# A two-layer diffusion backbone on one core: another order in the opening, at the layer boundaries and in the second mixing stage

## The chip, the core and the metric

The kernel runs on one core of a Trainium2 chip. The metric is the time of one execution on the device, in microseconds (us). Its median before the change is 2162.36 us over three runs (2161.0 to 2166.12).

## What is computed

Two streams of tokens pass through two layers: 256 latent tokens `x` (called X below) and 256 context tokens `ctx` (called H), each 1024 wide. The reference, cut to what matters:

```
for l in range(2):
    mod_x = silu(c) @ ada_w[l] + ada_b[l]        # 9 vectors of 1024: shifts, scales, gates
    mod_h = silu(c_ctx) @ ada_w[l] + ada_b[l]
    x, h += 0.5 * mod[2] * swiglu(modulated(x, h; mod, norm_g[l, 0]), ffa)
    sx, sh = mixer_streams(modulated(x, h; mod, norm_g[l, 1]), w_in[l], ...)
    x += mod_x[5] * mixer_output(sx, keys of h and x)   # MLA, differential attention, pooling, three gates
    h likewise, in layer 0 alone
    x, h += 0.5 * mod[8] * swiglu(modulated(x, h; mod, norm_g[l, 2]), ffb)   # h in layer 0 alone
return rmsnorm(x, final_g)

modulated(z) = rmsnorm(z, g) * (1 + scale) + shift
```

The change leaves all of this as it is; only the order of the work and some of its forms differ.

## The kernel before, in words

**Layout.** The residual stream lies as eight tiles `X[k]` of 128 features by 512 tokens; columns 0 to 255 (`XC`) are X, 256 to 511 (`HC`) are H. Every product is made in three passes from a high part and a low part of each operand (`mm3`, line 301): `wh*xh`, `wh*xl`, `wl*xh`. TensorE (PE) works through instructions in the order in which the program issues them, and so does every other engine.

**Weights.** Weights come from HBM as 406 chunks of 128x1024 (eight blocks of 128x128). `Weights.split` (line 152 and 156) loads a chunk, ACT rounds it to the high part `hi`, and POOL or DVE subtracts to get the low part `lo`. `k.pool_split(n)` says which of the two; the markers `P` and `D` in a schedule and `on_pool` set it. A ring holds four chunks.

**The opening** (`start`, from line 1420). The two conditioning rows are loaded into rows 0 and 1 of `crow` and go through Silu. PE makes three products of ones to have work (`warm`), transposes the rows into columns (`pa`), and broadcasts each row over 128 partitions by four products `cb` whose operands have two rows (line 1484). DVE and ACT square the tiles `X[k]` and add them; PE sums these over partitions (`total`, tile `pst`), the first slice of the modulation matrix is multiplied by the conditioning columns (`prod`, line 1508), ACT copies the broadcast rows to `cvec` (`wide`), DVE makes row products for the shifts (`shifts`, line 1519), and when the scales (`fin`), the root of the mean square (`rs`) and its broadcast `rB` are there, DVE and ACT make the modulated input (`ut` line 409, `uh` line 412, `ul` line 419). Then the first products `fg`, `fu` of the first FFN start (line 1578).

**The boundaries** (`boundary`, four of them: before each mixing stage, before the second FFN of layer 0, before the first FFN of layer 1). The last four output tiles of the stage before are finished for H first and then for X, so that H can be normalised while X is still being finished. `sqacc` squares an updated tile on ACT and adds it to `acc`, on POOL, and for the last tile on DVE (line 371). `stat` sums `acc` over partitions on PE (line 381, tile `pst`), ACT takes the root, DVE the reciprocal; `bcast` spreads it (line 396, `rB`). The next stage's first products ("items", `fg` and `fu` of the first two column groups of an FFN; `dk0`, `dq0`, `dv0` of a mixing stage) run for H alone: item 0 whole, then `xstat` for X, then item 1, with the broadcast and the modulation of X issued in its middle, then the rest; after that they run for X. A `W.hold` keeps their weights in the ring for the second pass.

**The mixing stages.** `SCHEDULE[l]` is an order written out by hand: twelve attention units in layer 1 (eight differential, four MLA), and behind each the names of the work that PE does before the next unit: projections (`dk`, `dq`, `kv`, `cq`, `q`, `k`), `v0`/`v1`, gates `g..`, transposes `T`, products with values `V`, statistics `ls` and `st` with `sq`, and `N` for a softmax step on DVE and POOL. A unit's scores (`sc`, lines 790 and 1118) fill four of the eight PSUM banks; DVE takes the maxima, ACT the exponentials, and then the banks are free.

Of the kernel before, what the change touches and what calls it, by code (L numbers as in the profile page):

```python
# [84 lines left out]
class Weights:  # L85


    def __init__(self, k, stream):
        self.k = k
        self.stream = stream  # L90
        self.c, self.off = -1, CW
        self.done = 0
        self.floor = None
        self.look = RING - 1
        self.hi, self.lo = {}, {}
        self.blocks = []
        self.early = {}
        self.jobs = [n for a, b in EARLY for n in range(a, b)]
        self.loaded = self.parted = None
        self.plain = 0  # L100

# [38 lines left out]
    def split(self, n, parts, copy):  # L140
# [13 lines left out]
        for p in range(parts):  # L154
            c = slice(p * CW // parts, (p + 1) * CW // parts)
            eng.tensor_tensor(out=lo[:, c], in0=raw[:, c], in1=hi[:, c].bitcast(F32), op=ALU.subtract)  # L156
# [6 lines left out]
    def prefetch(self, n, parts=1, copy=None):  # L163
        while self.done < NSPLIT and self.done <= n:
            self.split(self.done, parts, copy or self.k.nc.scalar.copy)
            self.done += 1
# [24 lines left out]
class Kernel:  # L191
# [274 lines left out]
    def boundary(self, l, i, specs, xs, update, head, func):  # L466
# [15 lines left out]
        for dm in g:  # L482
            banks[dm] = self.ps("dn")
            blks[dm] = self.gemm(banks[dm][:, HC], specs(dm), xs, HC)
            update(dm, banks[dm], HC)
            self.sqacc(dm, HC, nc.vector if dm == KD - 1 else None)
# [3 lines left out]
        for n, dm in enumerate(g):  # L490
            self.gemm(banks[dm][:, XC], blks[dm], xs, XC, mids[n])
            update(dm, banks[dm], XC)
            self.sqacc(dm, XC, nc.vector if dm == KD - 1 else None)
# [7 lines left out]
        def xstat():  # L501
            self.stat(X_)
            self.preload(func)
        for n, it in enumerate(items):
            it.mm(H_, lambda: (self.bcast(X_), self.mod_list(X_, range(KD)), self.mod_end()) if n == 1 else None)
            if n == 0:
                xstat()
# [920 lines left out]
    def start(self):  # L1428
# [6 lines left out]
        crow = self.pt("crow", F32).rearrange("p a b -> p (a b)")  # L1435
        nc.sync.dma_start(crow[0:2, :], cvec)
        nc.sync.dma_start(self.cst0, cst[:, 0:NK0])
# [45 lines left out]
        for (s, h), p in bc.items():  # L1483
            nc.tensor.matmul(p, self.ident[0:2, s:s + 1].to_broadcast([2, 128]), crow[0:2, h * 512:h * 512 + 512],
                             start=True, stop=True)

        def wide(s, copy):
            for h in range(2):
                copy(self.cvec[:, s, h * 512:h * 512 + 512], bc[s, h])
# [42 lines left out]
        for k in range(0, KD, 2):  # L1532
# [3 lines left out]
            if k == 2:  # L1536
                add(0, 2)
                total(0)
        prod(0, 1)
        wide(H_, act.copy)  # L1540
        dve.scalar_tensor_tensor(out=ab1, in0=self.v(V_ADAB + 8, 8), scalar=1.0, in1=self.v(V_NORM, 8),
                                 op0=ALU.add, op1=ALU.mult)
        total(4)
        turn(0, 1)
        total(6)
        shifts(0, H_)
        r, r2 = self.sm("rs", 4), self.sm("rs2", 4)
        act.activation(r, pst[:, 0:4], AF.Sqrt, scale=1.0 / D, bias=self.eps)
        dve.reciprocal(r2, r)
        wide(X_, act.copy)  # L1550
        fin(0, 1)
        p = self.ps("rB")
# [3 lines left out]
        shifts(0, X_)  # L1556
# [31 lines left out]
        self.W.prefetch(0)  # L1588
# [181 lines left out]
```

## Time and profile before

| | before |
|---|---|
| median of three runs | 2162.36 us |
| the profiled execution, its own time | 2161.61 us |
| its span, first to last instruction | 2159.8 us |
| mean granted clock of PE, as a share of full | 0.991 |
| PE busy | 2120.6 us (98%) |
| DVE, ACT, POOL busy | 63%, 42%, 36% |
| DMA, mean | 189 GB/s |

The span is what the trace covers; the profiled execution's own time is 1.8 us more. PE's busy time counts products that overlap, so 98% does not say that PE works at its peak; the 39 us in which it is not busy are real holes, and a stretch in which its granted clock is below 1.00 is slower work. In rows of instructions the columns are start, duration, engine, line, operation, tiles written and read, shapes, count; in brackets the idle time of that engine just before and what ended it.

### The profile page before, as it was taken

To read this page: it belongs to the slowest core of one execution; us is meant where nothing else is said; L and a number is where in the kernel's file an instruction comes from. 1 tells how busy PE (TensorE), PEld (TensorE's weight loads), DVE (VectorE), ACT (ScalarE), POOL (GpSimd) and SP (SyncE) were. 2 spreads that over 40 slices of the span, in tenths; PEclk is the share of its full clock that TensorE was granted. 3 is DMA by queue.
4 is the path that set the end of the run, shared out by engine and by line. 5 is a ranking of instruction groups with operands and counts; after the bars stand their busy time and mean duration, and the time that the engine had idled before them with its cause. 6 is when DMAs were issued, how large, how long until landed. Compare 5 with 4: busy or idle time off the path is not lost.

```text
span 2159.8 us, 31295 instructions
## 1 busy us (share of the span) xinstructions
PE 2120.6 (98%) x12032; PEld 1824.9 (84%) x12032; DVE 1370.3 (63%) x2016; ACT 899.7 (42%) x1529; POOL 772.2 (36%) x561
## 2 busy tenths in 40 slices
PE   9999999999999999999999999999999999999998
PEld 5888888977887788888888898888889888999998
DVE  6665655456656799468758745544534776667755
ACT  4433233345565533432212243332333557555544
POOL 0333324322475411555545544333343347301000
PEclk9999999999999999999999999999999999999999
DMA  7577767264322466245444515786664552455653
GB/s 265 184 292 278 256 265 273 86 217 142 113 93 80 150 234 234 88 145 181 172 166 166 175 69 209 294 299 237 264 246 147 205 185 79 166 200 191 229 183 115
DMA packets 119241, 408.91 MB, mean 189 GB/s; under 512 B 13234, under 2 KB 16946, under 8 KB 119092
## 3 DMA queue, kind: packets, MB, share of 16 engines
q1 hardware_dynamic: 103252, 354.48, 46.7%
q10 hardware_dynamic: 15840, 52.44, 6.2%
q8 instruction: 94, 1.54, 0.3%
q14 instruction: 55, 0.45, 0.1%
HBM read 348.67 MB, written 58.20 MB: 188 GB/s over the span
## 4 chain that ended last, share of the span: by engine, by line
PE 86%; DVE 6%; ACT 4%; issue 1%; DMA 1%; POOL 1%; ACTq 0%; DVEq 0%; SPq 0%; POOLq 0%
PE dn L301 22%; PE fu L301 19%; PE fg L301 19%; PE gt L301 8%; PE it L301 5%; PE br L301 5%; PE vi L301 2%; ACT pe L806 1%; DVE ul L419 1%; PE fg L1578 1%; PE fu L1578 1%; PE pa L1508 1%; PE tr L853 1%; PE sc L1118 1%; DMA X<-X 1%
## 5 line engine op out<-in xcount | busy, mean ns | idle before, releaser
L156 POOL TENSOR_TENSOR lo<-w,hi 128x1024 fp32r<-128x1024 f32 x204 | 530.4, 2603 | 701.3 <-ACT hi L152 652.9
L152 ACT CAST hi<-w 128x1024 fp32r<-128x1024 f32 x359 | 374.8, 1049 | 579.2 <-DMA w<-in_stream 237.6
L271 DVE CUSTOM_DVE_ANT_0 junk<-a,cvec 128x1024 bf16<-128x1024 f32 x224 | 400.5, 1788 | 3.7
L301 PE MATMUL dn<-hh,hi 128*128 128x512 f32 (+1 forms) x800 | 272.7, 341 | 0.0
L301 PE MATMUL dn<-hl,hi 128*128 128x512 f32 (+1 forms) x800 | 272.2, 340 | 0.0
L301 PE MATMUL dn<-hh,lo 128*128 128x512 f32 (+1 forms) x800 | 272.2, 340 | 0.0
L156 DVE TENSOR_TENSOR lo<-w,hi 128x1024 fp32r<-128x1024 f32 x155 | 190.5, 1235 | 127.9 <-ACT hi L152 125.5
L301 PE MATMUL fg<-ul,hi 128*128 128x512 f32 (+2 forms) x712 | 252.4, 354 | 1.6 <-DVE ul L419 1.6
L301 PE MATMUL fu<-uh,hi 128*128 128x512 f32 (+2 forms) x712 | 253.8, 357 | 0.0
L301 PE MATMUL fu<-ul,hi 128*128 128x512 f32 (+2 forms) x712 | 253.2, 356 | 0.0
L301 PE MATMUL fu<-uh,lo 128*128 128x512 f32 (+2 forms) x712 | 253.1, 355 | 0.0
L301 PE MATMUL fg<-uh,hi 128*128 128x512 f32 (+2 forms) x712 | 251.7, 354 | 0.0
L301 PE MATMUL fg<-uh,lo 128*128 128x512 f32 (+2 forms) x712 | 251.5, 353 | 0.0
L301 PEld LDWEIGHTS dn<-hh,hi 128*128 128x128 f32 x800 | 151.7, 190 | 17.0
L301 PEld LDWEIGHTS dn<-hl,hi 128*128 128x128 f32 x800 | 151.7, 190 | 16.8
L301 PEld LDWEIGHTS dn<-hh,lo 128*128 128x128 f32 x800 | 151.7, 190 | 16.9
L619 DVE SCALAR_TENSOR_TENSOR X<-dn,md,X 128x256 f32<-128x256 f32 x112 | 50.2, 479 | 170.6 <-PE dn L301 170.5
L301 PEld LDWEIGHTS fg<-ul,hi 128*128 128x128 f32 x712 | 134.4, 189 | 21.1 <-DVE ul L419 2.8
L301 PEld LDWEIGHTS fu<-uh,hi 128*128 128x128 f32 x712 | 136.4, 192 | 18.5
L301 PEld LDWEIGHTS fu<-ul,hi 128*128 128x128 f32 x712 | 136.4, 192 | 18.4
L301 PEld LDWEIGHTS fu<-uh,lo 128*128 128x128 f32 x712 | 136.2, 191 | 18.3
L301 PEld LDWEIGHTS fg<-uh,lo 128*128 128x128 f32 x712 | 134.5, 189 | 18.5
(321 smaller groups left out, 4303.2 us busy)
## 6 DMA issues: line engine op xcount, KB each, us to landing
w<-in_stream SPq DMA_DIRECT2D x359, 512.0 KB, 4.2
a<-in_ada SPq DMA_DIRECT2D x136, 512.0 KB, 4.4
el<-in_stream SPq DMA_DIRECT2D x47, 512.0 KB, 3.7
early<-eh ACTq DMA_DIRECT2D x47, 512.0 KB, 2.7
early<-el ACTq DMA_DIRECT2D x47, 512.0 KB, 3.7
hi<-early SPq DMA_DIRECT2D x47, 512.0 KB, 4.4
lo<-early SPq DMA_DIRECT2D x47, 512.0 KB, 5.8
a<-in_stream SPq DMA_DIRECT2D x8, 512.0 KB, 6.6
```

The lines of the kernel that those rows point to most:

```text
L152: copy(hi, raw)
L156: eng.tensor_tensor(out=lo[:, c], in0=raw[:, c], in1=hi[:, c].bitcast(F32), op=ALU.subtract)
L271: nc.vector.tensor_tensor_reduce(out=self.junk, in0=raw, in1=self.cvec[:, s, :], scale=1.0, scalar=0.0, op0=ALU.mult, op1=ALU.add, accum_o ...
L301: nc.tensor.matmul(out, a, b, start=first and n == 0, stop=last and n == 2)
L419: self.nc.vector.scalar_tensor_tensor(out=lo, in0=t, scalar=sh, in1=hi.bitcast(F32), op0=ALU.add, op1=ALU.subtract)
L619: nc.vector.scalar_tensor_tensor(out=x, in0=p[:, SC[s]], scalar=K.mod(self.l, m, s, dm), in1=x, op0=ALU.mult, op1=ALU.add)
L806: nc.scalar.activation(e[:, c], banks[i][:, c], AF.Exp, bias=nm[:, o:o + 1], scale=1.0, accum_out=ls[:, o:o + 1])
L853: nc.tensor.transpose(t[:, i * 128:i * 128 + 128], P[:, i * 128:i * 128 + 128], self.ident)
L1118: nc.tensor.matmul(out[qt], a[0:96, q0:q0 + 128], b[0:96, kc], start=n == 0, stop=n == 2)
L1508: nc.tensor.matmul(pa[0:2, c], ccol[:, 2 * i:2 * i + 2], ada[k, m][:, i * 128:i * 128 + 128], start=i == 0, stop=i == KD - 1)
L1578: nc.tensor.matmul(b, w[n // 2], x, start=k == n == 0, stop=k == KD - 1 and n == 2)
```

## The change

What it does, in the order of the program:

- `SCHEDULE[1]`, the order of the mixing stage of layer 1, is another one.
- `Weights.split` on POOL makes the low part in two halves of 128x512 (`parts=2`); on DVE it stays one instruction. In the opening the low part can be issued later than the high part (`lows`).
- `sqacc` for the last tile of a boundary no longer adds on DVE: the square stays apart (`sq7`) and `stat` sums both tiles on PE.
- `boundary`: where the first two items that take H are ordinary ones, they run together for H, block by block, with `xstat` after the sixth and the X broadcast and modulation after the eighth block. The boundary before layer 1's mixing has only one such item and keeps the old form.
- `start`: `crow` is zeroed (half on POOL, half on DVE) before its DMA, which is now behind that of `cst0`; the broadcasts `cb` use all 128 rows; two more `warm` products; the copies `wide`, the sums `total`, the X row product `shifts(0, X_)` and the rounding of the first chunk are issued earlier.

```diff
--- before.py
+++ after.py
@@ -48,11 +48,11 @@
...
-    "N dk1 dq1 | N P kv0 cq0 | N | N N N N N T kv1 N N N V D dk2 N N N dq2 N T N N N | N N cq1 | N cq2 dk3 N N P "
...
+    "dk1 dq2 N | N P N N N dq1 cq0 kv0 | P N T kv1 N | N N | dk2 N N N N D N N dk3 N N T N N dq3 cq1 N N N V N "
...
@@ -98,6 +98,7 @@
         self.jobs = [n for a, b in EARLY for n in range(a, b)]
         self.loaded = self.parted = None
         self.plain = 0
+        self.lows = None
 
     def plain_chunk(self, specs):
 
@@ -151,16 +152,24 @@
         nc.sync.dma_start(raw, self.stream[n])
         copy(hi, raw)
         eng = nc.gpsimd if k.pool_split(n) else nc.vector
-        for p in range(parts):
-            c = slice(p * CW // parts, (p + 1) * CW // parts)
-            eng.tensor_tensor(out=lo[:, c], in0=raw[:, c], in1=hi[:, c].bitcast(F32), op=ALU.subtract)
+        if eng is nc.vector:
+            parts = 1
+
+        def low():
+            for p in range(parts):
+                c = slice(p * CW // parts, (p + 1) * CW // parts)
+                eng.tensor_tensor(out=lo[:, c], in0=raw[:, c], in1=hi[:, c].bitcast(F32), op=ALU.subtract)
+        if self.lows is None:
+            low()
+        else:
+            self.lows.append(low)
         self.hi[n], self.lo[n] = hi, lo
 
     def pump(self):
         floor = self.c if self.floor is None else min(self.floor, self.c)
         self.prefetch(floor + self.look)
 
-    def prefetch(self, n, parts=1, copy=None):
+    def prefetch(self, n, parts=2, copy=None):
         while self.done < NSPLIT and self.done <= n:
             self.split(self.done, parts, copy or self.k.nc.scalar.copy)
             self.done += 1
@@ -483,14 +492,14 @@
             banks[dm] = self.ps("dn")
             blks[dm] = self.gemm(banks[dm][:, HC], specs(dm), xs, HC)
             update(dm, banks[dm], HC)
-            self.sqacc(dm, HC, nc.vector if dm == KD - 1 else None)
+            self.sqacc(dm, HC, False if dm == KD - 1 else None)
         mids = (None, lambda: (self.bcast(H_), self.mod_list(H_, (0, 1))),
                 lambda: self.mod_list(H_, (4, 5)), lambda: self.mod_end())
         ends = ((), (2, 3), (6, 7), ())
         for n, dm in enumerate(g):
             self.gemm(banks[dm][:, XC], blks[dm], xs, XC, mids[n])
             update(dm, banks[dm], XC)
-            self.sqacc(dm, XC, nc.vector if dm == KD - 1 else None)
+            self.sqacc(dm, XC, False if dm == KD - 1 else None)
             if n == 0:
                 self.stat(H_)
             self.mod_list(H_, ends[n])
@@ -501,10 +510,31 @@
         def xstat():
             self.stat(X_)
             self.preload(func)
-        for n, it in enumerate(items):
-            it.mm(H_, lambda: (self.bcast(X_), self.mod_list(X_, range(KD)), self.mod_end()) if n == 1 else None)
-            if n == 0:
-                xstat()
+        def xmods():
+            self.bcast(X_)
+            self.mod_list(X_, range(KD))
+            self.mod_end()
+        pair = [it for it in items if not isinstance(it, Kernel.VItem) and H_ in getattr(it, "streams", (H_,))][:2]
+        if len(pair) == 2:
+            preps = [it.prep(H_) for it in pair]
+            for it in pair:
+                it.blks = []
+            for k in range(KD):
+                for (out, sp, ys, cols), it in zip(preps, pair):
+                    it.blks.append(W.take(sp[k]))
+                    self.mm3(out, it.blks[k][:2], tuple(x[:, cols] for x in ys[k]), k == 0, k == KD - 1)
+                if k == 5:
+                    xstat()
+                elif k == 7:
+                    xmods()
+            for it in items:
+                if it not in pair:
+                    it.mm(H_)
+        else:
+            for n, it in enumerate(items):
+                it.mm(H_, xmods if n == 1 else None)
+                if n == 0:
+                    xstat()
         two = [it for it in items if not isinstance(it, Kernel.VItem)][:2]
         rest = [it for it in items if it not in two]
         preps = [it.prep(X_) for it in two]
@@ -1433,8 +1463,10 @@
         dve, act = nc.vector, nc.scalar
         xT, vec, cst, cvec = self.ins
         crow = self.pt("crow", F32).rearrange("p a b -> p (a b)")
+        nc.gpsimd.memset(crow[:, 0:512], 0.0)
+        dve.memset(crow[:, 512:1024], 0.0)
+        nc.sync.dma_start(self.cst0, cst[:, 0:NK0])
         nc.sync.dma_start(crow[0:2, :], cvec)
-        nc.sync.dma_start(self.cst0, cst[:, 0:NK0])
         one = self.pg("one")
         dve.memset(one, 1.0)
         pick = self.pick = self.cpool.tile([128, 7], F32, tag="pick", name="pick")
@@ -1481,8 +1513,9 @@
         for i in range(KD):
             nc.tensor.transpose(pa[:, 64 + 2 * i:66 + 2 * i], crow[0:2, i * 128:i * 128 + 128], self.ident[0:2, 0:2])
         for (s, h), p in bc.items():
-            nc.tensor.matmul(p, self.ident[0:2, s:s + 1].to_broadcast([2, 128]), crow[0:2, h * 512:h * 512 + 512],
+            nc.tensor.matmul(p, self.ident[:, s:s + 1].to_broadcast([128, 128]), crow[:, h * 512:h * 512 + 512],
                              start=True, stop=True)
+        warmup(1)
 
         def wide(s, copy):
             for h in range(2):
@@ -1536,24 +1569,27 @@
             if k == 2:
                 add(0, 2)
                 total(0)
+        total(4)
+        wide(H_, act.copy)
+        wide(X_, act.copy)
         prod(0, 1)
-        wide(H_, act.copy)
         dve.scalar_tensor_tensor(out=ab1, in0=self.v(V_ADAB + 8, 8), scalar=1.0, in1=self.v(V_NORM, 8),
                                  op0=ALU.add, op1=ALU.mult)
-        total(4)
+        total(6)
         turn(0, 1)
-        total(6)
+        warmup(1)
         shifts(0, H_)
         r, r2 = self.sm("rs", 4), self.sm("rs2", 4)
         act.activation(r, pst[:, 0:4], AF.Sqrt, scale=1.0 / D, bias=self.eps)
+        shifts(0, X_)
         dve.reciprocal(r2, r)
-        wide(X_, act.copy)
         fin(0, 1)
+        self.W.lows = []
+        self.W.prefetch(0)
         p = self.ps("rB")
         for j in range(4):
             nc.tensor.transpose(p[:, j * 128:j * 128 + 128], r2[:, j:j + 1].to_broadcast([128, 128]), self.ident)
         warmup(2)
-        shifts(0, X_)
         fin(0, 0)
         self.rB = {s: p[:, SC[s]] for s in (H_, X_)}
         self.mods[0, 0], self.mods[0, 1] = md
@@ -1585,7 +1621,8 @@
 
         for s in (H_, X_):
             self.modulate(0, s)
-        self.W.prefetch(0)
+        self.W.lows.pop()()
+        self.W.lows = None
         load(1, 1)
         load(1, 0)
         shifts(1, H_)
```

How the orders differ at three places. **PE in the opening**, from its first product to the first product of the FFN; before:

```order
L1447 MATMUL warm<-one 128x512 x3
L1482 MATMUL pa<-cst_75,crow 128x2 x8
L1484 MATMUL cb<-crow,cst_75 128x512 x4
L1499 MATMUL pst<-pick,sq 128x4 x4
L1508 MATMUL pa<-a_112,ccol 2x128 x8
L1499 MATMUL pst<-pick,sq 128x4 x4
L1516 MATMUL pa<-cst_75,row 128x2
L1499 MATMUL pst<-pick,sq 128x4 x4
L1554 MATMUL rB<-cst_75,rs_188 128x128 x4
L1447 MATMUL warm<-one 128x512 x2
L1578 MATMUL fg<-uh_203,hi_226 128x512
```

and now:

```order
L1479 MATMUL warm<-one 128x512 x3
L1514 MATMUL pa<-cst_75,crow 128x2 x8
L1516 MATMUL cb<-crow,cst_75 128x512 x4
L1479 MATMUL warm<-one 128x512
L1532 MATMUL pst<-pick,sq 128x4 x8
L1541 MATMUL pa<-a_114,ccol 2x128 x8
L1532 MATMUL pst<-pick,sq 128x4 x4
L1549 MATMUL pa<-cst_75,row 128x2
L1479 MATMUL warm<-one 128x512
L1591 MATMUL rB<-cst_75,rs_194 128x128 x4
L1479 MATMUL warm<-one 128x512 x2
L1614 MATMUL fg<-uh_212,hi_199 128x512
```

The second sum moved ahead of `prod`, one `warm` product now stands behind `cb` and one ahead of `rB`. The line numbers of the changed file are 32 to 37 higher here.

**PE at the boundary before the second FFN of layer 0**, around the statistics of X (`pst`); `uh5` to `uh7` are the last tiles of the modulated H input, `hi137` and `hi138` chunks of weights; before, between the first item and the second:

```order
L301 MATMUL fg_8196<-uh7_8078,hi137_8043 128x256
L301 MATMUL fg_8196<-ul7_8079,hi137_8043 128x256
L301 MATMUL fg_8196<-uh7_8078,lo137_8044 128x256
L381 MATMUL pst_8227<-pick_84,acc_7805 128x2 x2
L301 MATMUL fu_8236<-uh0_8064,hi138_8111 128x256
```

and now, inside the joint loop over both items:

```order
L310 MATMUL fg_8274<-uh5_8151,hi138_8188 128x256
L310 MATMUL fg_8274<-ul5_8152,hi138_8188 128x256
L310 MATMUL fg_8274<-uh5_8151,lo138_8189 128x256
L310 MATMUL fu_8275<-uh5_8151,hi138_8188 128x256
L310 MATMUL fu_8275<-ul5_8152,hi138_8188 128x256
L310 MATMUL fu_8275<-uh5_8151,lo138_8189 128x256
L390 MATMUL pst_8319<-pick_86,acc_7877 128x2 x2
L390 MATMUL pst_8319<-pick_86,sq_8272 128x2 x2
L310 MATMUL fg_8274<-uh6_8153,hi138_8188 128x256
```

The statistics moved from behind the eighth block of one item to behind the sixth block of two, and consist of two pairs instead of one.

**ACT in the mixing stage of layer 1**, around the squares `sq` of the differential outputs `od`, which PE sums in `st`; before, behind the exponentials `pe` of the third MLA unit:

```order
L1140 ACTIVATE pe_15768,ls_15763<-sc_15746,nm_15762 128x512
L1140 ACTIVATE pe_15770,ls_15763<-sc_15747,nm_15762 128x512
L1140 ACTIVATE pe_15772,ls_15763<-sc_15754,nm_15762 128x512
L1140 ACTIVATE pe_15774,ls_15763<-sc_15755,nm_15762 128x512
L952 ACTIVATE sq_15776<-od0_14127 128x256
L952 ACTIVATE sq_15777<-od1_14128 128x256
L952 ACTIVATE sq_15778<-od2_14129 128x256
L952 ACTIVATE sq_15779<-od3_14130 128x256
L349 ACT_TABLE_LOAD
```

and now:

```order
L1170 ACTIVATE pe_15877,ls_15866<-sc_15858,nm_15865 128x512
L914 COPY pv_15902<-po_15885 64x512
L982 ACTIVATE sq_15906<-od0_14329 128x256
L982 ACTIVATE sq_15907<-od1_14330 128x256
L982 ACTIVATE sq_15908<-od2_14331 128x256
L982 ACTIVATE sq_15909<-od3_14332 128x256
L349 CAST pth_15919<-tr_15914 128x4x128
L349 CAST pth_15919<-tr_15923 128x4x128
```

The squares moved ahead of the transposed probabilities `pth` of an earlier unit, and of the third unit's exponentials. On PE a gate of 24 products now stands between that unit's scores and `st`.

## Rows read from the trace of the kernel before

**Rows 1.** The page's first part: busy time of each engine.

```profile
PE 2120.6 (98%) x12032; PEld 1824.9 (84%) x12032; DVE 1370.3 (63%) x2016; ACT 899.7 (42%) x1529; POOL 772.2 (36%) x561
```

**Rows 2.** Waits of PE, whole run: who waited for whom, total us, times, longest.

```profile
PE pst L381 <- DVE acc L371: 7.5, 4, 2.7
PE sc L1118 <- ACT qh L343: 3.6, 1, 3.6
PE st L961 <- ACT sq L952: 2.1, 1, 2.1
...
PE br L301 <- DVE odl L341: 1.1, 1, 1.1
PE it L301 <- DVE pdl L341: 1.1, 1, 1.1
```

**Rows 3.** Opening by stretches: busy per engine, PE's granted clock, DMA share, GB/s.

```profile
8.00:10.00 2.00, 2.00 (x6) 0.82 (x5) 1.78 (x4) 1.23 (x2) 0.00 (x0) 1.00 1.03 379
...
12.00:14.00 2.00, 2.00 (x11) 1.73 (x12) 1.90 (x4) 0.00 (x0) 0.00 (x0) 0.50 1.03 418
...
22.00:24.00 2.00, 1.55 (x2) 0.00 (x0) 0.99 (x3) 1.84 (x5) 0.00 (x0) 0.51 0.58 205
```

**Rows 4.** Timeline of PE in the opening.

```profile
7.38 4.29 PE L1484 MATMUL cb<-crow,cst 2*128 2x512 f32 x8
...
13.40 3.57 PE L1508 MATMUL pa<-a,ccol 128*2 128x128 f32 x16
...
20.24 3.31 PE L1447 MATMUL warm<-one 128*128 128x512 f32 x4
24.11 0.50 PE L1578 MATMUL fg<-uh,hi 128*128 128x512 f32 x1 [0.55 <-ACT hi L152]
...
25.70 1.91 PE L1508 MATMUL pa<-a,ccol 128*2 128x128 f32 x16
```

**Rows 5.** Timeline of DVE and of ACT in the opening.

```profile
20.49 1.23 DVE L1519 CUSTOM_DVE_ANT_0 junk<-a,cvec 128x1024 bf16<-128x1024 f32 x1 [0.79 <-ACT cvec L1489]
...
23.02 1.98 ACT L152 CAST hi<-w 128x1024 fp32r<-128x1024 f32 x2
```

**Rows 6.** The four boundaries, one stretch each; columns as in rows 3.

```profile
402.00:412.00 10.00, 8.16 (x62) 7.36 (x61) 6.78 (x14) 4.48 (x9) 2.38 (x2) 1.00 0.48 176
...
897.00:912.00 15.00, 11.46 (x66) 10.67 (x65) 9.91 (x16) 7.15 (x13) 7.60 (x4) 0.77 0.31 105
...
1268.00:1282.00 14.00, 10.47 (x64) 9.67 (x63) 8.91 (x16) 6.72 (x12) 6.97 (x4) 0.76 0.40 151
...
1637.00:1651.00 14.00, 12.16 (x95) 11.36 (x94) 9.32 (x19) 5.97 (x13) 2.74 (x2) 1.00 0.36 133
```

**Rows 7.** Timeline of DVE and of POOL at the second boundary.

```profile
902.89 2.12 DVE L371 TENSOR_TENSOR acc<-acc,sq 128x256 f32<-128x256 f32 x1 [0.61 <-ACT sq L367]
...
902.38 4.84 POOL L156 TENSOR_TENSOR lo<-w,hi 128x1024 fp32r<-128x1024 f32 x2 [1.35 <-ACT hi L152]
```

**Rows 8.** Timeline of PE there: the statistics of H and the product behind.

```profile
888.43 0.51 PE L381 MATMUL pst<-pick,acc 128*128 128x2 f32 x4
888.80 0.36 PE L301 MATMUL dn<-mh,hi 128*128 128x256 f32 x1
```

**Rows 9.** Timeline of POOL before the second boundary: one instruction of 128x512.

```profile
875.92 1.29 POOL L371 TENSOR_TENSOR acc<-acc,sq 128x512 f32<-128x512 f32 x1 [1.79 <-ACT sq L367]
```

**Rows 10.** Timeline of DVE in layer 1's mixing: maxima of the sixth unit, then `ls`.

```profile
1719.15 2.47 DVE L799 TENSOR_REDUCE nm<-sc 128x1 f32<-128x512 f32 x4
...
1725.83 3.34 DVE L915 RECIPROCAL r<-r 2x512 f32<-2x512 f32 x1
```

**Rows 11.** Timeline of PE there: the sixth unit's scores, and the wait.

```profile
1715.17 0.50 PE L790 MATMUL sc<-dk2h,dq2h 32*128 32x512 f32 x4
...
1729.22 1.12 PE L938 MATMUL rb<-r,cst 2*128 2x512 f32 x2 [1.18 <-DVE r L915]
```

**Rows 12.** A stretch of an FFN; columns as in rows 3.

```profile
100.00:200.00 100.00, 100.00 (x443) 82.81 (x442) 61.34 (x73) 37.41 (x45) 35.07 (x14) 1.00 0.77 294
```

8 rows, old and new, of the table SCHEDULE are left out of this document.

## The prediction

> **What bounds the kernel.** The page comes first: PE is busy for 2120.6 of 2159.8 us and no other engine for more than 63% [rows 1]. In an FFN stretch it has no hole at all: 443 instructions in 100 us at full clock, 0.226 us each [rows 12]. So an edit that only lightens DVE, ACT or POOL there is worth nothing; what can be won is the 39 us of holes and the places where PE works at a lower granted clock. The waits of PE name the largest holes [rows 2]: four times the statistics of a boundary wait for a DVE addition, 7.5 us together, then single waits of the second mixing stage. Windows show the clock [rows 3, 6]: full (2.4 GHz) at 8 to 10 us, half (1.2 GHz) at 12 to 14 and at 22 to 24, and a mean of 0.77 and 0.76 at the second and third boundary, against 1.00 at the first and fourth. The change touches just these three places, and I take them one by one. The sum is made against the profiled execution, 2161.61; the median of the runs is 0.75 above it.
>
> **Opening.** The four broadcasts `cb` now multiply 128 rows, 126 of them zeros, instead of two. Before, PE was busy without a hole from 8 to 17 us, yet its clock fell from 1.00 to 0.50 while the products `cb` on two rows ran (7.38 to 11.67) [rows 3, 4]. Everything behind them was paid double until the clock rose at about 17 us: `prod` took 3.57 us for sixteen records, and the same sixteen take 1.91 at full clock later [rows 4]. If `cb` on 128 rows keeps the clock, `prod` gives back 1.66 us, and the statistics behind it less than that. On the way to the first FFN product `fg`, which began at 24.11, stood also the X row product, 1.23 us, only started at 20.49, after a copy of ACT that now runs earlier, and the rounding `hi`, two chunks at 23.02 for 1.98 us, for which `fg` waited 0.55 [rows 4, 5]. Both move ahead of the modulation; `fg` is then limited by `uh`.
>
> Against that: one `warm` product more behind `cb` and one ahead of `rB`. Two of them took 3.31 us at half clock [rows 4], so one costs some 0.83 at full; both stand where PE would wait for DVE and ACT anyway, and if that cover is gone they cost 1.7. The zeroing of `crow` (128x512, once on POOL, once on DVE) is not in the trace. Nearest is POOL's addition on 128x512, 1.29 us [rows 9]; as its DMA has to wait for it, I take 0.45 of delay, between 0 and 1.3. I put `fg` at 21 to 22 us. Not all of the 2 to 3 us stays: the inputs of the second block depend on a low part that DVE makes after the first modulation, and when that chain doesn't move as far, PE waits there. **Term: −2.5 us, between −0.5 and −4.**
>
> **Boundaries.** In the windows [rows 6] idle time is what is missing in PE's busy column, and lost time is one minus the clock, times the length: 10 − 8.16 = 1.84 at the first; 15 − 11.46 = 3.54 idle and 0.23 × 15 = 3.45 lost at the second; 3.53 and 0.24 × 14 = 3.36 at the third; 1.84 at the fourth. The cause at the second is in the timelines [rows 7]: DVE's addition of the last square took 2.12 us at 902.89, for 128x256, because POOL worked at its two low parts from 902.38 on, 4.84 us for both. The statistics waited for that addition, and the clock fell behind the hole. Now that addition is gone; `stat` waits for the square on ACT and for older sums on POOL only.
>
> The second gain is in the pair. Two items in one loop give 6 products instead of 3 for each block of H, so a modulated tile `ul` may come twice as late; and the X statistics come after 36 products instead of 24, at some 0.12 us each for 256 columns (half of 0.226). X then has about 24 × 0.12 = 2.9 us of cover behind the statistics ahead of its broadcast, in the blocks seven and eight and the next. So I take the holes at the second and third boundary as closed and the clock as kept, and leave the first a third of its hole. The fourth has one ordinary item that takes H, keeps the old form, and loses only the wait for DVE.
>
> The price: each of eight statistics gets two more products of two columns. Four records at 888.43 delayed the next product to 888.80 [rows 8], 0.37; so 0.74 a boundary. Together: −1.84 + 0.74 = −1.1; −3.54 − 3.45 + 0.74 = −6.25; −3.53 − 3.36 + 0.74 = −6.15; and at the fourth, where the wait for DVE is about 1.0 of the 1.84, −0.3. **Term: −14 us, between −6 (the holes closed by half, the clock still down) and −15.**
>
> **Mixing of layer 1.** The squares for `st` now stand earlier on ACT, and 24 gate products cover them: the wait of 2.1 goes [rows 2]. The row sums `rb` waited 1.18 for a reciprocal at 1729.22. It ended at 1725.83 + 3.34 = 1729.17; the maxima had begun at 1719.15, 4 us after the scores at 1715.17 [rows 10, 11], for DVE worked for other steps until then. In the new order a gate stands ahead of that unit and not `dq3`, so the maxima may begin with the scores; I leave 0.3 of the wait, −0.9. `br` waited 1.1 for `odl` [rows 2]; a gate now stands behind `dn2` and covers it, −1.1. The largest wait, 3.6 for `qh` [rows 2], stays: the same exponentials and roundings stand ahead of `qh` on ACT, and POOL's low part on POOL. `it` waited 1.1 for `pdl` [rows 2]; between `pp0` and `pj0` now stands one gate where more stood, some 3 us less cover, and I charge +0.5 there. A few new half-microsecond waits are as likely as not. **Term: −4 us, between +3 and −7.**
>
> **The low parts in halves.** POOL makes about 205 chunks; a chunk takes 2.42 (half of 4.84) [rows 7], in halves twice 1.29 [rows 9], so about 0.2 more each, some 40 us of POOL, which is idle for nearly two thirds of the span. It costs nothing as long as a chunk is ready before PE wants it; a chunk serves 24 products of 0.226 = 5.4 us [rows 12]. The gain, DVE held for one half at most, is in the boundary term already. **Term: 0.**
>
> Sum: −2.5 − 14 − 4 = −20.5 against 2161.61, so 2141.1 for a profiled execution and about **2142** as a median. A measurement of this kernel can tell some 0.3%, 6.5 us, from no change.
>
> **The rivals.**
>
> *A. The clock doesn't care how many rows a broadcast has.* The clock could follow only whether PE is busy; then `cb` on 128 rows changes nothing, the stretch to 17 us stays at half clock, and the two added products cost 1.66 each. Only the moved row product and rounding help: `fg` at about 23.6, a gain of 0.5, and 2144 in all. Against it speaks that before `cb` PE was just as busy, at full clock [rows 3]. The Trainium skill (TensorE: Matmul & The Clock Gate, section "What's actually happening") says that a hardware block sets the clock by how busy PE has been recently. Taken literally it gives this rival, and the trace doesn't agree with that reading, since PE was busy 2.00 of 2.00 us with the clock at 0.50.
>
> *B. The second mixing order gives back what it wins.* Units that follow each other closely fill the PSUM banks, and a projection waits for exponentials; two such waits as long as that for `qh` (3.6) would turn −4 into about +4: 2150.
>
> *C. The boundaries keep their clock.* If the wait for DVE becomes one for the square or for POOL's sums, a hole remains, the clock falls as before, and only half of the −14 is there: 2149.
>
> *D. POOL's halves come late, and the kernel is slower.* The place is wherever DVE works beside POOL: an addition of 128x256 was stretched to 2.12 there [rows 7]. With halves the two engines can alternate. If each half is held for two DVE instructions of about 1.23 [rows 5], a chunk takes 2 × (1.29 + 2.46) = 7.5 us, against the 5.4 in which PE uses one. At 2.1 us a chunk this decides from 13 chunks on (13 × 2.1 = 27 us, 2169); with 20 of the 205 it would be 2184. Held for one DVE instruction each, a chunk takes 5.04, under 5.4, and nothing is lost. As long as POOL and its ring are ahead, none of it shows.
>
> **How the numbers follow.** The forecast, with all three gains near their size, 0.63; A 0.14; B 0.12; C 0.08; D 0.03. The range goes from 2134 (the boundaries at −15, mixing at −7 and the opening at −4 give −26, so 2136.4, with 2 us for what is not in the sum) to 2151, which takes in A, B and C. Faster by more than 0.3% means under 2155.9, and A, B and C are all there: 0.93, which leaves them room to come together; same 0.05; slower 0.02, a part of D.
>
> **What would show it.** In the opening: clock 1.00 through 10 to 17 us and `fg` at 21 to 22; clock 0.50 there is A. At the boundaries: no wait of `pst` for DVE, and windows of the second and third boundary at 1.00 with under 1 us idle; a clock of 0.8 is C. In the mixing stage: no wait for `sq`, that for `qh` still near 3.6, and `it` for `pdl` a little longer; a new wait of `tr` or `sc` above 2 us is B. A row of PE waits for POOL's `lo` is D. The forecast is wrong if the PE holes fall by less than 8 us in all, or if the time is above 2151.

## The result, and the profile after

The changed kernel takes 2137.76 us (median of four runs, 2135.98 to 2140.31) against 2162.24 for the kernel before, now over four runs (2161.0 to 2166.12): a ratio of 0.9885, 95% interval 0.9868 to 0.9902, 24.5 us less. Its profiled execution took 2135.98 with a span of 2134.2, so 25.6 less than that of before. The prediction was 2142, within 2134 to 2151.

The page's first part, and the longest waits of PE, answer to [rows 1, 2]:

```profile
PE 2110.2 (99%) x12068; PEld 1821.0 (85%) x12068; DVE 1297.5 (61%) x2008; ACT 899.4 (42%) x1530; POOL 883.5 (41%) x768
```

```profile
PE sc L1148 <- ACT qh L352: 3.8, 1, 3.8
PE it L310 <- ACT pdh L349: 2.1, 1, 2.1
PE warm L1479 <- DVE pick L1473: 2.0, 1, 2.0
PE rb L968 <- DVE r L945: 1.4, 1, 1.4
PE it L310 <- ACT pe L836: 1.3, 1, 1.3
```

The wait of the statistics for DVE's addition, 7.5 us, is gone, and so is that of `st` for the squares, 2.1; `qh` stays, and the projection that waited 1.1 for `pdl` now waits 2.1 for `pdh`, the high part of the same tile. PE's holes fell from 39.2 to 24.0 us (2134.2 − 2110.2). That is 15 of the 25.6. Much of the rest is clock: its mean rose from 0.991 to 0.997, so what is lost to it fell by some 13 us (0.009 × 2159.8 against 0.003 × 2134.2). The two overlap, since some of the low clock falls into holes. The opening after, by windows and on PE's timeline (columns as in rows 3 and 4):

```profile
8.00:10.00 2.00, 2.00 (x6) 0.83 (x5) 1.86 (x3) 0.63 (x1) 0.00 (x0) 1.00 0.99 352
...
12.00:14.00 2.00, 2.00 (x18) 1.90 (x17) 1.79 (x4) 0.78 (x2) 0.00 (x0) 1.00 1.02 416
```

```profile
7.68 3.70 PE L1516 MATMUL cb<-crow,cst 128*128 128x512 f32 x8
...
13.93 1.91 PE L1541 MATMUL pa<-a,ccol 128*2 128x128 f32 x16
...
20.11 0.50 PE L1614 MATMUL fg<-uh,hi 128*128 128x512 f32 x1
```

At 12 to 14 us the clock is 1.00 where it was 0.50, the row product takes 1.91 instead of 3.57, and the first FFN product starts 4.0 us earlier [rows 3, 4]. The three boundaries with a pair, from the first product for H on, have neither a hole nor a low clock, against [rows 6]:

```profile
398.75:410.00 11.25, 11.25 (x97) 11.25 (x96) 7.38 (x19) 6.01 (x12) 2.11 (x2) 1.00 0.41 151
890.80:910.00 19.20, 19.20 (x163) 19.20 (x162) 10.12 (x25) 11.08 (x19) 9.51 (x8) 1.00 0.24 83
1254.60:1274.00 19.40, 19.40 (x165) 19.40 (x164) 10.18 (x25) 11.24 (x19) 9.71 (x8) 1.00 0.31 109
```

To split the 25.6 us I take the same instruction in both traces: the first product of the statistics of H at each boundary, and the first product behind the 48 for H (at the fourth boundary the next `it` behind the item `it` and the values `vi`). Each row is a stretch, with the time at which it ends.

| stretch | ends, before | ends, after | gained | forecast |
|---|---|---|---|---|
| opening and first FFN, to H's statistics | 393.06 | 389.00 | 4.06 | 2.5 |
| boundary 1 | 411.69 | 405.53 | 2.10 | 1.1 |
| mixing of layer 0 | 888.43 | 881.05 | 1.22 | 0 |
| boundary 2 | 911.58 | 897.58 | 6.62 | 6.25 |
| second FFN of layer 0 | 1258.80 | 1244.88 | −0.08 | 0 |
| boundary 3 | 1281.18 | 1261.41 | 5.85 | 6.15 |
| first FFN of layer 1 | 1628.40 | 1608.71 | −0.08 | 0 |
| boundary 4 | 1649.93 | 1628.99 | 1.25 | 0.3 |
| mixing of layer 1, last FFN, end | 2159.8 | 2134.2 | 4.66 | 4 |

The mixing of layer 1 stands in one window each, all its holes inside, first before, then after:

```profile
1650.00:1860.00 210.00, 197.92 (x1387) 173.86 (x1387) 147.68 (x263) 118.60 (x272) 101.28 (x122) 0.98 0.47 165
```

```profile
1650.00:1860.00 210.00, 200.03 (x1441) 178.79 (x1442) 144.41 (x259) 124.92 (x277) 104.86 (x137) 0.98 0.48 165
```

Idle time fell from 12.1 to 10.0 us, 2.1 of the 4.66. In windows of 10 us before has three with a clock of 0.83, after two: 1.7 more. The remaining 0.9 was not traced. How far such a split can be trusted is seen where two profiles share the work. Run e11 below is the kernel before up to the mixing of layer 1: its mixing of layer 0 took 474.08 us, where the profile of before has 476.74 (888.43 − 411.69). Run e1 differs from the changed kernel in the opening alone: from boundary 4 to its end it took 508.78, where the changed kernel has 505.21. A gain of 1 to 3 us in a mixing stage is within that. The boundaries are steadier: in e11 the first three take 18.64, 22.77 and 21.84 us, where the profile of before has 18.63, 23.15 and 22.38.

### The profile page after: what moved, and what is told of

Its sections match the earlier page's. It is cut to its first block, busy times and chain, and to the rows that moved or that the text cites. A ratio compares the mean times of both kernels' runs of the same rounds, so it can differ in the third digit from the quotient of the medians.

```text
span 2134.2 us, 31733 instructions
## 1 busy us (share of the span) xinstructions
PE 2110.2 (99%) x12068; PEld 1821.0 (85%) x12068; DVE 1297.5 (61%) x2008; ACT 899.4 (42%) x1530; POOL 883.5 (41%) x768
## 4 chain that ended last, share of the span: by engine, by line
PE 90%; ACT 4%; DVE 4%; issue 1%; POOL 1%; DMA 0%; ACTq 0%; DVEq 0%; POOLq 0%
PE dn L310 22%; PE fg L310 19%; PE fu L310 19%; PE gt L310 8%; PE it L310 7%; PE br L310 5%; PE vi L310 2%; ACT pe L836 1%; PE fg L1614 1%; PE fu L1614 1%; PE tr L883 1%; PE pa L1541 1%; PE sc L1148 1%; PE po L907 1%; ACT pe L1170 1%
## 5 line engine op out<-in xcount | busy, mean ns | idle before, releaser
L161 POOL TENSOR_TENSOR lo<-w,hi 128x512 fp32r<-128x512 f32 x410 | 644.7, 1597 | 583.2 <-ACT hi L153 552.7
L280 DVE CUSTOM_DVE_ANT_0 junk<-a,cvec 128x1024 bf16<-128x1024 f32 x224 | 350.6, 1565 | 3.7
L610 DVE TENSOR_TENSOR h<-sg,fu 128x512 f32<-128x512 f32 x66 | 45.2, 686 | 189.0 <-PE fu L310 110.8
```

The lines of the kernel that those rows point to most:

```text
L280: nc.vector.tensor_tensor_reduce(out=self.junk, in0=raw, in1=self.cvec[:, s, :], scale=1.0, scalar=0.0, op0=ALU.mult, op1=ALU.add, accum_o ...
L610: nc.vector.tensor_tensor(out=h[:, c], in0=sg[:, c], in1=pu[:, c], op=ALU.mult)
```

## The experiments

Each run stands beside the kernel before, run with it (medians 2162.93, 2164.04 and 2163.15); gains are against that, and ratios carry their 95% interval.

**The rows of the broadcasts, taken back.** In the changed kernel, `cb` on two rows again:

```diff
-nc.tensor.matmul(p, self.ident[:, s:s + 1].to_broadcast([128, 128]), crow[:, h * 512:h * 512 + 512],
+nc.tensor.matmul(p, self.ident[0:2, s:s + 1].to_broadcast([2, 128]), crow[0:2, h * 512:h * 512 + 512],
```

> The changed kernel, only its four broadcasts back on two rows. If the rows of the broadcasts hold the clock: it falls to 0.50 while they run, the row product behind takes some 3.5 us instead of 1.91, and the first FFN product starts 2 to 3.5 us later than at 20.11, so about 2140 to 2141 in all. If the clock follows only whether PE is busy, or if the added warm product and the new order hold it: clock 1.00 from 8 to 17 us, first FFN product at 20.1 within 0.3, the time unchanged (2138).

2143.62 us, ratio to before 0.9904 (0.9884 to 0.9924). Windows, and PE's timeline:

```profile
8.00:10.00 2.00, 2.00 (x7) 0.94 (x6) 1.79 (x4) 0.98 (x3) 0.00 (x0) 1.00 1.00 355
...
16.00:18.00 2.00, 2.00 (x11) 1.76 (x11) 1.20 (x2) 0.00 (x0) 0.00 (x0) 0.50 1.03 412
```

```profile
7.93 4.37 PE L1516 MATMUL cb<-crow,cst 2*128 2x512 f32 x8
...
17.45 3.57 PE L1541 MATMUL pa<-a,ccol 128*2 128x128 f32 x16
25.31 0.50 PE L1614 MATMUL fg<-uh,hi 128*128 128x512 f32 x1
```

PE is busy without a hole in both, and only the rows of `cb` differ: the clock falls and `fg` starts 5.2 us later, 0.25 of it because `cb` itself started later. That is later even than before the change. So the rows decide, and by more than I gave them.

**The rows alone**, in the kernel before (the reverse of that edit, the zeroing of `crow`, and its DMA behind that of `cst0`):

> The kernel before, only with the four broadcasts on 128 rows (and the zeroing that they need). If the rows hold the clock: 1.00 from 8 to 17 us, the row product 1.91 instead of 3.57, and the first FFN product 2 to 3 us earlier than at 24.11, since what follows waits for that product. If the clock follows only whether PE is busy: 0.50 at 12 to 16 us as before, and the first FFN product at 24.1 to 24.6, for the zeroing delays it.

2158.68 us, ratio 0.9982 (0.997 to 0.9993). The clock is 1.00 through 8 to 18 us. On PE's timeline:

```profile
20.98 0.50 PE L1580 MATMUL fg<-uh,hi 128*128 128x512 f32 x1 [1.97 <-ACT hi L152]
```

3.1 us earlier than [rows 4], and now it waits 1.97 for the rounding, where it waited 0.55: what the next run moves.

**The whole opening alone**, in the kernel before (its `start`, and the late low part):

> The kernel before with the whole opening of the change and nothing else. If the four places add up: the first FFN product at 20.1 and the first boundary's statistics of H 4.1 us earlier than at 393.06, so about 2158 in all, with the waits of the boundaries as before (7.5 us for the addition on DVE). If the gain of the opening is lost again in the first FFN: that statistics within 1 us of 393.06.

2159.24 us, ratio 0.9981 (0.997 to 0.9992).

```profile
19.82 0.50 PE L1593 MATMUL fg<-uh,hi 128*128 128x512 f32 x1
```

`fg` is 4.3 us earlier, and the first boundary's statistics start at 388.69, 4.4 earlier: all of it arrives.

**The boundary alone**, in the kernel before: the square apart, and the pair.

> The kernel before with the boundary of the change alone: the last square apart, and the two first items together for H. If these two edits alone close the holes: no wait of pst for DVE, the second and third boundary 6 us shorter each with clock 1.00, about 2147 to 2149 in all. If the halves on POOL are needed as well (a whole low part of 2.4 us holds DVE or the squares' sums on POOL): a hole of over 1 us stays at the second and third boundary, and the time is 2151 or more.

2147.32 us, ratio 0.992 (0.9904 to 0.9936), some 17 us. PE waits neither for DVE's addition nor at the second and third boundary:

```profile
896.00:912.00 16.00, 16.00 (x136) 16.00 (x135) 10.54 (x25) 10.32 (x18) 5.63 (x4) 1.00 0.30 99
1260.00:1276.00 16.00, 16.00 (x136) 16.00 (x135) 10.43 (x25) 10.45 (x18) 5.54 (x3) 1.00 0.39 133
```

So the halves on POOL are not needed for these two. In its trace the first three boundaries are 2.1, 6.6 and 5.8 us shorter than before, as in the table; the fourth is 1.0 longer.

**The square apart alone**:

```diff
-self.sqacc(dm, HC, nc.vector if dm == KD - 1 else None)
+self.sqacc(dm, HC, False if dm == KD - 1 else None)
...
-self.sqacc(dm, XC, nc.vector if dm == KD - 1 else None)
+self.sqacc(dm, XC, False if dm == KD - 1 else None)
```

> The kernel before with the last square apart only; the items still run one after the other. If the addition on DVE was the whole cause: no wait of pst over 0.5 us, clock 1.00 at the second and third boundary, 9 to 12 us less, about 2151. If the statistics, 24 products in, come too early without it as well: pst then waits for the square on ACT or for POOL's sum, the waits for ul of 0.8 us a boundary stay, the clock still falls at the second and third boundary, and the gain is under 6 us.

2152.6 us, ratio 0.9947 (0.9927 to 0.9967), 11.5 us. The windows of [rows 6], second and third boundary, and what is left of the waits:

```profile
897.00:912.00 15.00, 14.44 (x116) 13.74 (x115) 11.64 (x24) 9.32 (x19) 7.71 (x4) 1.00 0.31 106
1268.00:1282.00 14.00, 13.94 (x118) 13.85 (x117) 7.22 (x17) 7.02 (x13) 4.67 (x2) 1.00 0.33 115
```

```profile
PE fg L301 <- DVE ul L419: 0.9, 4, 0.3
PE it L301 <- DVE ul L419: 0.9, 4, 0.3
```

No wait for the statistics, and the clock stays at 1.00, with 24 products ahead of them, not 36. Holes of 0.2 to 0.3 us for `ul` are left. The second and third boundary take 18.11 us each, against 23.15 and 22.38 before, 16.59 in the run above and 16.53 in the changed kernel.

**The pair alone**, the last square still added on DVE:

> The kernel before with the two items together only; the last square still added on DVE. If the cover of 12 more products is enough by itself: 36 products, 4.5 us, against some 5.7 us from the start of the items to the end of the addition, so pst still waits 1 to 1.5 us at the second and third boundary but ul no longer; the clock stays 1.00 where the hole is under about 1.5 us, 8 to 11 us less in all. If the hole decides whatever its length: the clock falls as before, 3 to 5 us less.

2160.99 us, ratio 0.9984 (0.9975 to 0.9993).

```profile
PE pst L381 <- DVE acc L371: 7.9, 4, 2.8
```

```profile
899.45 2.11 DVE L371 TENSOR_TENSOR acc<-acc,sq 128x256 f32<-128x256 f32 x1 [0.61 <-ACT sq L367]
```

The wait is as long as before, and DVE's addition still held, 2.11 us. My expectation took 5.7 us from the first product to the end of the addition; before it was 905.01 − 897.73 = 7.3 [rows 7], so 36 products (4.5 us) cannot cover it.

**POOL's halves alone**, in the kernel before (`parts=2` for POOL):

> The kernel before with POOL's low parts in halves and nothing else. If the halves only shorten how long POOL holds DVE: DVE's addition at the second and third boundary takes under 1.8 us instead of 2.12, the waits of pst for it fall from 7.5 to 4 to 6 us, the waits of layer 0's mixing for exponentials and transposes fall by 1 us, and the time by 0 to 5 us. If the halves come late for PE: a wait of PE for a low part of POOL shows, and the time is 2166 or more.

2150.48 us, ratio 0.9931 (0.9912 to 0.9949), 13.6 us, far more than I gave them. PE's wait, and DVE's addition at the second boundary beside POOL's half:

```profile
PE pst L383 <- DVE acc L373: 5.2, 4, 1.6
```

```profile
898.81 1.03 DVE L373 TENSOR_TENSOR acc<-acc,sq 128x256 f32<-128x256 f32 x1 [0.61 <-ACT sq L369]
```

```profile
898.29 1.26 POOL L158 TENSOR_TENSOR lo<-w,hi 128x512 fp32r<-128x512 f32 x1 [1.34 <-ACT hi L152]
```

The addition takes 1.03 us instead of 2.12 [rows 7]: it ends at 899.84, just behind the half that had begun at 898.29 and ended at 899.55. Before, it ended at 905.01, behind the first of POOL's two low parts, which ended at some 904.80 (902.38 and half of 4.84). The waits for `ul` went too. But the hole is not closed, and the clock still falls:

```profile
890.00:910.00 20.00, 18.41 (x142) 18.24 (x141) 15.62 (x34) 12.57 (x23) 10.76 (x9) 0.91 0.31 106
```

The second and third boundary take 19.02 and 19.06 us.

**The halves taken back**, in the changed kernel (`parts=1`):

> The changed kernel with POOL's low parts whole again. If the halves and the square kept apart remove the same holes (each alone brought 11 to 14 us): hardly slower, 2138 to 2141, the boundaries without a wait of pst for DVE and with clock 1.00, and only the waits of layer 0's mixing come back (about 1 us). If the halves have a gain of their own that adds up: 2146 or more, with new holes at places where DVE is held by a whole low part.

2137.25 us, ratio 0.9876 (0.9844 to 0.9908): no slower than the change. The second and third boundary:

```profile
890.00:910.00 20.00, 20.00 (x170) 20.00 (x169) 11.09 (x26) 11.92 (x20) 9.04 (x6) 1.00 0.27 85
1254.00:1274.00 20.00, 19.83 (x167) 19.74 (x166) 10.49 (x26) 11.92 (x20) 8.83 (x5) 1.00 0.34 111
```

So at these two boundaries the halves and the square apart go for the same hole, and where the square is apart and the items are paired the halves bring nothing more. At the fourth boundary two waits for `ul` of 0.2 and 0.3 us are back and it takes 20.97 us, not 20.28. Layer 0's mixing did not become longer again (474.12).

**The pair taken back**, in the changed kernel (the old loop over the items):

> The changed kernel with the old order of the boundary's items: the first whole for H, then the statistics of X, then the second. If the square apart and the halves already close the holes: pst waits under 0.5 us and ul not at all, clock 1.00, the time 2137 to 2140. If the pair is needed as cover: each of the three boundaries with a pair loses 1.5 to 2 us to waits for ul, for the square or for the reciprocal, 2142 to 2146.

2140.1 us, ratio 0.9884 (0.9857 to 0.9911). From the statistics of H to the end of the 48 products at the second boundary it takes 899.73 − 882.34 = 17.39 us instead of 16.53: 0.9 for the pair, and as much at the first and third, half of what the second theory wanted. Some 0.8 us more arose in layer 0's mixing, of which neither theory speaks; the clock was 0.87 and 0.96 there in two stretches of 10 us, from 506 on. The medians are 2.3 apart, their runs overlap, and the ratios are the same.

**The order of the second mixing stage alone**, in the kernel before:

> The kernel before with the new order of the second mixing stage and nothing else. If the order by itself brings the term: the time from the X statistics of the fourth boundary to the end is 4 to 4.5 us shorter than before, no wait of st for squares, one of 3.6 to 3.9 us for qh, 2157 to 2159 in all. If the stage gained only because DVE is held less: under 2 us shorter.

2157.95 us, ratio 0.9979 (0.9962 to 0.9995), some 4.5 us, between 1 and 8. In the trace, though, the way from the fourth boundary's X statistics to the end is only 2.2 us shorter (2153.9 − 1639.77 against 2159.8 − 1643.44), between the two theories. Its holes are nearly those of the changed kernel, but the clock behind the two longest is not; first this run, then the changed kernel:

```profile
1780.00:1790.00 10.00, 8.20 (x39) 7.51 (x40) 7.33 (x15) 5.87 (x16) 5.66 (x9) 0.66 0.00 0
1840.00:1850.00 10.00, 7.97 (x34) 6.70 (x34) 6.91 (x13) 4.50 (x10) 3.28 (x2) 0.66 0.35 118
```

```profile
1760.00:1770.00 10.00, 6.22 (x31) 5.08 (x31) 7.95 (x16) 5.47 (x14) 6.18 (x8) 0.83 0.00 0
1820.00:1830.00 10.00, 7.80 (x46) 6.93 (x45) 6.93 (x13) 5.39 (x13) 6.10 (x7) 0.83 0.36 126
```

0.34 × 10 = 3.4 us lost behind each hole here, 0.17 × 10 = 1.7 there. So the term of this stage is not one number: 2 us of holes, and some us of clock that differ between executions.

**Further than the change: `q3` ahead of its unit.** In the changed kernel two names swapped:

```diff
-k0 q4 q0 q2 g41 T N V p3 V N k1 ma N | mb q3 T q5 k2
+k0 q3 q0 q2 g41 T N V p3 V N k1 ma N | mb q4 T q5 k2
```

> The changed kernel with two names of the second mixing order swapped: the projection q3 ahead of the first MLA unit, q4 behind it. If the wait of 3.8 us for qh comes from q3 being queued on ACT behind that unit's exponentials: the wait goes or falls under 1 us, the half clock behind it (0.83 in 1760 to 1770) too, and the time falls by 4 to 6 us to 2132 to 2134. If what holds qh is POOL's low part, or the next unit then waits for q4 instead: a wait of over 2 us stays there or one unit later, and the time stays at 2136 to 2138.

2137.93 us, ratio 0.9882 (0.9863 to 0.99). The wait for `qh` is gone, and this one is new:

```profile
PE tr L883 <- POOL pe L1179: 3.8, 1, 3.8
```

The second theory: the next transposes wait as long for the probabilities that POOL normalises.

**Cover moved there as well**: `p1` ahead of these transposes, `pj3` between `pp0` and `pj0`.

```diff
-N V sq T N p1
+N V sq p1 T N
...
-pj2 T pj3 N pp0 g00 om2 pj0
+pj2 T N pp0 g00 pj3 om2 pj0
```

> The changed kernel with three moves in the second mixing order: q3 ahead of the first MLA unit and q4 behind it (as in the run before), p1 ahead of the transposes that then waited 3.8 us for POOL, and pj3 behind g00 ahead of pj0. If those 24 products each are cover that was only at the wrong place: the transposes wait 0.8 us instead of 3.8, the wait of 2.1 for pdh goes, and the clock stays full behind both, 5 to 8 us less, 2130 to 2133. If ACT, DVE and POOL set the pace of the units there: the waits turn up at the next scores or transposes, and the time stays within 2 us of 2138.

2136.29 us (2135.76 to 2137.41), ratio 0.9868 (0.9842 to 0.9895): 1.5 below the change's median, which these runs cannot tell from none. The longest waits inside the stage:

```profile
PE st L991 <- DVE st L989: 1.5, 1, 1.5
PE rb L968 <- DVE r L945: 1.4, 1, 1.4
PE tr L883 <- POOL pe L1179: 0.9, 1, 0.9
PE it L310 <- DVE pdl L350: 0.9, 1, 0.9
```

The transposes wait 0.9 as expected, and `pdh` no longer, but `st` waits 1.5 for DVE in their place. PE's idle time between 1750 and 1790 is 5.1 us (4.5 in the changed kernel). What was waited for is spread, not removed, as the second theory has it.

## Why the prediction was right

**Opening, −2.5: right mechanism, too small.** It was 4.06, just past the end of its range. "`prod` gives back 1.66 us, and the statistics behind it less than that" was mis-sized: in the new order with the broadcasts on two rows, everything from the second half of `cb` to 21 us is paid double, some 5 us at `fg`. The delay that I charged for the zeroing, 0.45, does not stand out: `cb` started at 7.38 before and at 7.68 after, but at 6.74 to 7.66 in the six profiles without the zeroing and at 6.76 to 8.16 in the eight with it. What I held back for the second block was not needed: its `uh` started 4.7 us earlier (32.15 to 27.46). The size is partly luck: in three other profiles with the old opening the statistics of boundary 1 came at 394.5 to 394.8 and not at 393.06, and against those the gain would be 5.5 to 5.8. *Rival A* falls: with PE busy 2.00 of 2.00 us in both, the clock was 0.50 with two rows and 1.00 with 128. The Trainium skill (TensorE: Matmul & The Clock Gate, section "What's actually happening") says that how busy PE has been recently sets the clock; read as the time in which instructions run, that does not agree with these two runs, and the measurement decides. Whether rows of zeros or the number of rows as such count was not tried.

**Boundaries, −14: 15.8.** The second and third were within 0.4 us of their terms. The two small ones were forecast too short, for two reasons. PE's busy column undercounts a hole: at the first boundary 24 products and the statistics took 408.53 − 402.36 = 6.17 us before; at 0.12 and 0.37 they need 3.25. That is 2.92 lost, where the column shows 1.84 [rows 6]: each of the three holes cost about 0.26 more, since a product counts as busy for 0.28 where the next could start after 0.12, and the one behind a hole holds up its successor; some 0.3 are delays for `ul` that left no hole. And the fourth, 1.25, has a part that I had put at nothing without looking: with the square apart alone it takes 20.97 us against 21.53, and only the halves bring it to 20.28, by the waits for `ul`. My text left the first boundary a third of its hole, and my sum did not; the hole closed. The price of the two added products was nearly right: 0.81 us for both pairs (403.07 to the next product at 403.88), against 0.37 to 0.44 before.

The step that failed, without harm to the sum, is the division of the gain: "the second gain is in the pair". At the second boundary the square apart alone gives 5.0 of the 6.6 us (23.15 to 18.11). The pair alone leaves the wait for DVE and brings some 3 us in the whole run; on top of the square it brings 1.5 a boundary without the halves (18.11 to 16.59), and 0.9 with them. *Rival C* does not show: no hole at the three boundaries with a pair, clock 1.00.

**Halves, 0: right as a part of this sum, wrong as a price.** POOL's time, by lines, before and after:

```profile
L156 POOL TENSOR_TENSOR lo<-w,hi 128x1024 fp32r<-128x1024 f32 x204 | 530.4, 2603 | 701.3 <-ACT hi L152 652.9 <-PE fg L301 25.9 <-PE fu L301 9.6
```

```profile
L161 POOL TENSOR_TENSOR lo<-w,hi 128x512 fp32r<-128x512 f32 x410 | 644.7, 1597 | 583.2 <-ACT hi L153 552.7 <-PE fu L310 14.6 <-DMA w<-in_stream 6.9
```

114 us more, where I had 40: a half takes 1.60 on the mean, not 1.29. DVE's busy time fell by 73 us in return (1370.3 to 1297.5). So it looks as if a half now waits for DVE where DVE waited for it; that is read from the sums, not from single rows. PE never waits for a low part of POOL, so *rival D* does not show. But the halves alone are worth 13.6 us; I had put that gain in the boundary term, which was right but for 0.7 us at the fourth boundary, and had not seen how large it is by itself. In the trace of that run the four boundaries give 10.9 of it.

**Mixing of layer 1, −4: 4.66 to the end, by partly other waits, and with luck.** My parts came to −3.6. `st` and `br` went, `qh` stayed at 3.8, and `pdh` grew by 1.0 (I charged 0.5). A wait of before that I had not counted went as well:

```profile
PE tr L853 <- ACT pe L806: 1.6, 1, 1.6
```

Against that, a projection waits 1.3 for exponentials, and `rb` did not fall to 0.3 but rose to 1.4. After, on PE, DVE and PE:

```profile
1698.74 0.51 PE L820 MATMUL sc<-dk2h,dq2h 32*128 32x512 f32 x4
1700.25 2.48 DVE L829 TENSOR_REDUCE nm<-sc 128x1 f32<-128x512 f32 x4
1710.32 1.12 PE L968 MATMUL rb<-r,cst 2*128 2x512 f32 x2 [1.43 <-DVE r L945]
```

The maxima do begin sooner behind the scores, 1.5 us against 4.0 [rows 10, 11]. But PE also comes to `rb` sooner: its hole begins at 1708.89 (1710.32 − 1.43), 10.15 us behind the scores, against 1728.04 (1729.22 − 1.18), 12.87 behind them [rows 11]. So the cover shrank with the chain. That is the step of this term that failed. *Rival B* is this in small; it did not decide. That the sum fits is partly the clock, 1.7 us, which the order alone did not keep and which run e1, with the same order, did not have either: its 508.78 us would have made the term 1.1.

**Not in the sum, and no gain:** 1.2 us in layer 0's mixing, whose order is the same. Two runs that are the changed kernel up to layer 1's mixing, e4 and e12, took 474.25 and 474.24 us there, and run e11, which is the kernel before up to there, took 474.08. So equal work differs by up to 2.7 us between executions, and the profile of before happened to be long. Why stays open; in e6 and e10 a clock of 0.86 to 0.97 over 20 us is part of it.

The parts add up: by their ratios the opening alone gives 4, the boundary alone 17 and the order alone 4.5, together 26, where the change's ratio gives 25. Their intervals, 2.4 to 3.6 us to either side, are too wide for this to be a proof. The halves' 13.6 is not a fourth part.

## What to carry to other kernels

Ask of two fixes whether they close the same hole before adding them: here half-length instructions on POOL and one addition less on DVE went for the same hole, each took most of it alone, and together they were not worth their sum. Price a hole on TensorE from the starts of the instructions around it, and add what the granted clock shows behind it. When a run of products with few rows stands at the head of a chain, look at the clock of what follows: filling the rows with zeros was worth 3 to 5 us here.

## What was not expected of the hardware

The clock fell with TensorE busy without a hole, after products over two rows, and stayed at 1.00 with the same work over 128 rows. The same instructions cost different clock in different executions: with the old opening, `fg` started at 24.1 us in three profiles and at 25.6 to 25.8 in three, and holes of the same kind in the second mixing stage were followed by a loss of 1.7 us in one and 3.4 in another. An addition of 128x256 on DVE took 2.12 us beside a whole low part on POOL and 1.03 beside halves.
